# Routing of a mixture-of-experts layer: GpSimd's share moved to VectorE, the first tile's ranks moved behind the second tile's heads

## The chip, the cores and the metric

The kernel runs on one core of a Trainium2 chip. The metric is the device time of one execution, in microseconds (us); the median of several runs is compared. A core has five engines with instruction streams of their own: TensorE (PE in the profile; PEld is its weight load), VectorE (DVE), ScalarE (ACT), GpSimd (POOL) and SyncE (SP), whose queue issues most of the loads. Each takes its instructions in the order of the program; they wait for each other by semaphores.

## The reference

Two transformer blocks in a row, each of two layers, on 256 tokens of width 1024, in float32. The first (retention and stick-breaking attention, SwiGLU) is not touched. Of a layer of the second this matters:

```python
x = layer_norm(DEEPNORM_ALPHA * x + mix, ln1_g[l], ln1_b[l])     # mix: three attentions, then w_o
moe = hier_moe(x, router_group_w[l], ...)
x = layer_norm(DEEPNORM_ALPHA * x + moe, ln2_g[l], ln2_b[l])

def hier_moe(...):
    lg = einsum('td,dg->tg', t, rg_w) + rg_b                      # 4 groups
    g_hot = one_hot(argmax(lg)); p_top = sum(softmax(lg) * g_hot)
    le = einsum('td,gde->tge', t, re_w) + re_b                    # 8 experts in each group
    top_v, top_i = lax.top_k(le of the group, 2)
    gate = g_hot * (p_top * softmax(top_v) at top_i)
    for g in range(4):
        h = silu(t @ w_gate[g]) * (t @ w_up[g])
        y = y + (h * gate) @ w_down[g]
```

## The kernel before

The 256 tokens are two tiles of 128 (`t` = 0, 1; NT = 2). Matrix products with large weights are three matmuls each (`mm3`, lines 189 to 191: weights split in a high part `whi` and a low part `wlo`, tokens in `hi` and `lo`).

`mix2` computes the attentions of a layer. Its last part runs over the two tiles: the heads of the dilated attention in two pairs (`dil_pair`: products of queries and keys on line 897, a masked map with its row sum on VectorE on line 900, exponentials on ScalarE on line 905, the scaling of the shares on line 649, transposes on line 652, products with the values on line 917), then the out-projection into two accumulators `acc` of 512 columns, eight steps `k` of three matmuls each (and one matmul with `alpha` times the old `h`, line 947). The matmuls of an out-projection that have their inputs early are issued among the heads' steps, as fillers for TensorE's waits.

Then layer norm 1 and the routing of the tile. `nrm.stat` takes the statistics of each `acc` (line 675). `rt.logits` copies `acc` to `raw` on ScalarE (line 1016), transposes it (line 252) and multiplies with the router's weights (line 1031); the norm is applied to the 40 logits afterwards. `rt.route` works on VectorE (lines 1055 to 1077): maximum, group, top two experts, and `sg`, whose first half marks the two experts of each token. `rt.rank` counts the tokens of each expert with a matmul with a triangular matrix (`strict`, line 1123; for tile 1 also `ones`, line 1122, on the marks of tile 0), and `rt.places` (line 1114) turns the ranks into the 0/1 matrix `P` that gathers tokens into the slots of the experts, 32 for each.

The function `rest` of a tile does the remainder: `features` normalizes `acc` into `h` and, in the transposed order that the gather wants, into `hi` (ScalarE, lines 1039 and 1040), and takes `lo` = `h` - `hi` on GpSimd (line 1041); `nrm.affine` multiplies `h` by the gain and adds the bias (line 693, the first 512 columns on GpSimd, the others on VectorE), and `gates` computes the gate weights (lines 1087 to 1101). For tile 0 it runs inside the loop, for tile 1 after `mix2`.

`moe` then gathers the tokens of each group of experts (`group`, matmuls on line 1178, taken out of PSUM into `xe` on lines 1048 and 1050), counts the tokens of the fullest expert (`rt.count`, read into registers by the engines as `most_i`, line 1340), and runs through eight steps, each with four experts: gate and up products (line 1206), hidden values (line 1226), down products. The expert weights are 96 tiles of 1 MB a layer, loaded on SP's queue in order (line 1161) into every buffer that has come free, among them `rowb`, the 1 MB that holds gain and bias of layer norm 1, and `raw`, `whi`, `wlo`, `wx`, `more`.

Pools and a scheduler set the order of the instructions on each engine out of the order of the code; `keep_in_program_order` holds an instruction at its place in the code, and `issue_after` keeps instructions behind a given one.

Of the kernel before, what the change touches and what calls it, by code (L numbers as in the profile page):

```python
# [29 lines left out]
PIECES = 4  # L30

# [71 lines left out]
def tile_fn(ctx: ExitStack, tc: tile.TileContext, a: dict, out: bass.AP, stop=None, start=1):  # L103
# [560 lines left out]
    class LayerNorm:  # L664
# [19 lines left out]
        def shift(self, mv, y):  # L684
            nb = sm.tile([128, 1], F32, name="lnb")
            nc.vector.scalar_tensor_tensor(nb, mv[:, 0:1], -1.0, y, op0=OP.mult, op1=OP.mult)
            return nb
# [25 lines left out]
    def mix2(l, xp, wx, x, last, tabs, rt, ahead):  # L713
# [237 lines left out]
        for t in range(NT):  # L951
            pair = [dil_pair(t, n) for n in range(2)]
            for n in (0, 1, 0, 1) if t == 0 else (0, 0, 1, 1):
                next(pair[n])
            for k in (0, 2, 4):
                for c in range(2):
                    out_proj(t, c, range(k, k + 2))
            for c in range(2):
                out_proj(t, c, range(6, 8))
                nrm.stat(t, c, acc[t, c])  # L960
            rt.logits(t, [acc[t, c] for c in range(2)])
            mv, y = nrm.stats(t)
            rt.route(t, mv, y)
            rt.rank(t)
            rt.first.append(rt.places(rt.ranks(t, 0, 2)))
            after = (t, [acc[t, c] for c in range(2)], y, nrm.shift(mv, y))

            def rest(t=t, after=after):
                rt.features(*after)
                nrm.affine(t, 0, nc.gpsimd)  # L970
                nrm.affine(t, 1, nc.vector)
                rt.gates(t)
            if t == 0:
                rest()
        return rest
# [3 lines left out]
    class Route:  # L979
# [32 lines left out]
        def logits(self, t, src):  # L1012

            raw = [self.xp.tile([128, 512], F32, name="raw", tag="dt", bufs=2) for c in range(2)]
            for c in range(2):
                nc.scalar.copy(raw[c], src[c])
            for c in range(2):
                self.half(t, c, raw[c])

        def half(self, t, c, r):  # L1020
# [7 lines left out]
            if c:  # L1028
                self.acc = ps.tile([128, 512], F32, name="rt", tag="at", bufs=PB["at"])[:, :NR]
                for k in range(8):  # L1030
                    nc.tensor.matmul(self.acc, self.xT[2 * t + k // 4][:, k % 4], self.rw[:, k], start=k == 0, stop=k == 7)

        def features(self, t, src, y, nb):


            hi, lo = self.xt[t] = new_x(t)
            for c in range(2):
# [3 lines left out]
                nc.gpsimd.tensor_tensor(lo[:, :, sp], h[t][:, sl].rearrange("t (p k) -> t k p", k=8), hi[:, :, sp].bitcast(F32), op=OP.subtract)  # L1041
# [76 lines left out]
        def rank(self, t):  # L1118

            rk = ps.tile([128, 512], F32, name="rk", tag="at", bufs=PB["at"])[:, :NE]  # L1120
# [4 lines left out]
            nc.vector.scalar_tensor_tensor(self.rk[t], self.sel[t], -1024.0, rk, op0=OP.mult, op1=OP.add)  # L1125

# [10 lines left out]
    def moe(l, xp, wx, rt, then, ahead):  # L1137
# [31 lines left out]
        def gather(xe, P, n, tags, label=None):  # L1169

            nk, todo = 8 // len(tags), []
            for i, tag in enumerate(tags):
                todo.append((i * nk, ps.tile([128, nk, n], F32, name=tag, tag=tag, bufs=PB[tag])))
            for t in range(NT):
                for k0, pg in todo:
                    for k in range(nk):
# [157 lines left out]
        for i in range(NU):  # L1334
            q = i % 2
            if q == 0:
                xe, PT, gs, rest = group(i // 2)
                if i == 0:
                    rt.count()
            most = nc.values_load(rt.most[0:1, i:i + 1], min_val=0, max_val=T, skip_runtime_bounds_check_because="a count of tokens")  # L1340
            xq, gq = xe[:, :, q * 128:(q + 1) * 128], gs[:, q:q + 1]
            if i < NU - 1:
# [6 lines left out]
                hq = gate_up(i, xq, gq, others, None if i else rest)  # L1349
# [70 lines left out]
    for l in range(DEPTH):  # L1420
# [9 lines left out]
        rest()  # L1430
        if stop == f"at{l}":
            return store()
# [12 lines left out]
        with tc.tile_pool(name=f"moe{l}", bufs=1) as xp:  # L1445
            moe(l, xp, wx, rt, then, ahead)
# [32 lines left out]
```

## Time and profile before

| | us |
|---|---|
| median of 3 runs | 1728.81 (1728.62 to 1729.09) |
| the profiled execution | 1728.63 |
| its span (first to last instruction) | 1726.8 |
| outside the span | 1.83 |
| mean granted TensorE clock, share of full speed | 0.946 |
| TensorE busy | 1578.6 (91%) |
| VectorE busy | 906.1 (52%) |
| ScalarE busy | 680.9 (39%) |
| GpSimd busy | 80.3 (5%) |

The busy shares are means over 1727 us with very different stages: the first block and the projections keep TensorE busy throughout, the two MoE stages (about 1064 to 1260 and 1488 to 1680) move weights at some 418 GB/s. The change lies in two stretches of some 60 us, one ahead of each MoE stage, so they are read from a timeline and from windows. A row of a timeline begins with start and duration; a last part in brackets says how long the engine had stood idle, and what ended that.

### The profile page before, as it was taken

What the parts mean: (1) busy time and instruction counts of PE and PEld (TensorE: products, weight loads), DVE (VectorE), ACT (ScalarE), POOL (GpSimd) and SP (SyncE); (2) the same over time, 40 slices, a digit from 0 to 9 for tenths busy, and PEclk for the clock granted to TensorE, in tenths of its full rate; (3) what the DMA queues carried; (4) which work ended last, traced back from release to release, by engine and by line L of the source; (5) the groups of instructions that cost most, each with busy time, mean ns of one, the idle gap of its engine ahead of it and who ended that gap; (6) DMA issues with size and microseconds to landing.
All of it is one profiled execution on the core that took longest, in us unless ns stands there. A gap on an engine that the chain in (4) does not pass through costs nothing. (4 is left out here: it accounts for less than half of the span.)

```text
span 1726.8 us, 24247 instructions
## 1 busy us (share of the span) xinstructions
PE 1578.6 (91%) x9468; PEld 1190.1 (69%) x9468; DVE 906.1 (52%) x1966; ACT 680.9 (39%) x1126; POOL 80.3 (5%) x102
## 2 busy tenths in 40 slices
PE   9999999999999999999999998777779999786785
PEld 8788888888878888888787775443358777443442
DVE  5757675545575666445478544222167845432132
ACT  6543454343644445434376633111036754211010
POOL 0000000000000000000300111000030011100000
PEclk9999999999999999999999988988889998898798
DMA  9354546465635455546445628999972744899992
GB/s 321 123 193 149 193 163 204 154 213 181 207 122 194 154 185 174 187 143 223 139 124 190 225 102 341 418 418 419 413 256 87 255 160 168 357 417 419 419 372 71
DMA packets 133988, 399.54 MB, mean 231 GB/s; under 512 B 8133, under 2 KB 36805, under 8 KB 110278
## 3 DMA queue, kind: packets, MB, share of 16 engines
q1 hardware_dynamic: 130096, 390.62, 62.2%
q10 hardware_dynamic: 3734, 6.82, 1.1%
q8 instruction: 97, 1.59, 0.4%
q14 instruction: 61, 0.50, 0.1%
HBM read 396.37 MB, written 1.05 MB: 230 GB/s over the span
## 5 line engine op out<-in xcount | busy, mean ns | idle before, releaser
L165 DVE TENSOR_TENSOR wlo<-raw,whi 128x2048 fp32r<-128x2048 f32 (+6 forms) x314 | 405.8, 1310 | 306.7 <-ACT whi L164 305.8
L189 PE MATMUL acc<-whi,x 128*128 128x512 f32 (+3 forms) x1248 | 484.6, 389 | 0.2 <-ACT x L243 0.2
L164 ACT CAST whi<-raw 128x2048 fp32r<-128x2048 f32 (+7 forms) x346 | 355.1, 1063 | 325.2 <-PE acc L191 273.4
L191 PE MATMUL acc<-whi,x 128*128 128x512 f32 (+3 forms) x1248 | 478.6, 384 | 0.1
L190 PE MATMUL acc<-wlo,x 128*128 128x512 f32 (+3 forms) x1248 | 478.4, 384 | 0.0
L189 PEld LDWEIGHTS acc<-whi,x 128*128 128x128 f32 x1248 | 237.7, 190 | 45.1 <-issue 4.3
L190 PEld LDWEIGHTS acc<-wlo,x 128*128 128x128 f32 x1248 | 237.8, 191 | 44.3 <-issue 4.1
L191 PEld LDWEIGHTS acc<-whi,x 128*128 128x128 f32 x1248 | 237.3, 190 | 43.3 <-issue 2.3
L1206 PE MATMUL at<-whi,xe 128*32 128x256 f32 x448 | 105.4, 444 | 18.8 <-DMA whi<-in_expert_w_gate_dram 14.8
L1226 DVE SCALAR_TENSOR_TENSOR hq<-hh,gs,at 128x256 f32<-128x256 f32 x16 | 10.5, 656 | 167.5 <-PEq L1351 114.1
L1206 PE MATMUL at<-wlo,xe 128*32 128x256 f32 x416 | 84.4, 423 | 8.4 <-ACTq L1346 4.0
L165 POOL TENSOR_TENSOR wlo<-raw,whi 128x416 fp32r<-128x416 f32 (+1 forms) x32 | 32.8, 1059 | 1062.3 <-ACT whi L164 1062.2
L190 PE MATMUL acc<-wlo,fh 128*128 128x512 f32 x176 | 70.0, 398 | 0.0
L191 PE MATMUL acc<-whi,fl 128*128 128x512 f32 x176 | 70.0, 397 | 0.0
L189 PE MATMUL acc<-whi,fh 128*128 128x512 f32 x176 | 69.9, 397 | 0.0
L1206 PE MATMUL at<-wx,xe 128*32 128x256 f32 x416 | 51.3, 429 | 17.7 <-PEq L1317 6.7
L1206 PEld LDWEIGHTS at<-whi,xe 128*32 128x32 f32 x448 | 43.4, 126 | 34.0 <-issue 16.4
L1239 ACT COPY hT<-ph 128x256 f32<-128x256 f32 x17 | 6.3, 372 | 151.6 <-PE ph L1233 142.8
L244 DVE TENSOR_TENSOR yl<-acc,yh 128x512 fp32r<-128x512 f32 x30 | 20.6, 687 | 86.3 <-ACT yh L243 86.3
L1206 PE MATMUL at<-more,xe 128*32 128x256 f32 x352 | 55.0, 443 | 11.2 <-DMA more<-in_expert_w_up_dram 6.8
L1206 PE MATMUL at<-raw,xe 128*32 128x256 f32 x320 | 52.5, 474 | 12.8 <-issue 5.7
L1206 PEld LDWEIGHTS at<-wlo,xe 128*32 128x32 f32 x416 | 35.1, 120 | 24.8 <-issue 7.7
(378 smaller groups left out, 2192.0 us busy)
## 6 DMA issues: line engine op xcount, KB each, us to landing
raw<-in_w_in_dram SPq DMA_DIRECT2D x55, 1024.0 KB, 5.2
raw<-in_w_gate_up_dram SPq DMA_DIRECT2D x40, 1024.0 KB, 5.2
raw<-in_w_down_dram SPq DMA_DIRECT2D x22, 1024.0 KB, 4.9
whi<-in_expert_w_gate_dram SPq DMA_DIRECT2D x16, 1024.0 KB, 14.0
raw<-in_w_in_dram SPq DMA_DIRECT2D x28, 512.0 KB, 4.1
wx<-in_expert_w_up_dram SPq DMA_DIRECT2D x14, 1024.0 KB, 17.4
wx<-in_expert_w_down_dram SPq DMA_DIRECT2D x14, 1024.0 KB, 7.1
wlo<-in_expert_w_up_dram SPq DMA_DIRECT2D x14, 1024.0 KB, 17.4
```

The source lines that it names most:

```text
L164: nc.scalar.copy(hi[:, s], raw[:, s])
L165: eng.tensor_tensor(lo[:, s], raw[:, s], hi[:, s].bitcast(F32), op=OP.subtract)
L189: nc.tensor.matmul(acc, xhi[:, kt], whi[:, k, c0:c1], start=first, stop=False)
L190: nc.tensor.matmul(acc, xhi[:, kt], wlo[:, k, c0:c1], start=False, stop=False)
L191: nc.tensor.matmul(acc, xlo[:, kt], whi[:, k, c0:c1], start=False, stop=last)
L244: nc.vector.tensor_tensor(lo, p, hi.bitcast(F32), op=OP.subtract)
L1206: nc.tensor.matmul(pu[r], xe[:, k, r], W[i][4 * m + u][:, k], start=k == 0, stop=k == 7, skip_group_check=True)
L1226: nc.vector.scalar_tensor_tensor(hq.rearrange("s k p -> s p k"), hh.rearrange("s (p k) -> s p k", k=2), gs, pu.rearrange("s (p k) -> s p k ...
L1239: nc.scalar.copy(hT, ph)
```

## The change

In the loop of `mix2`: the last out-projection steps of both halves come first, then `logits`, and the statistics read the copy `raw` in SBUF in place of `acc` in PSUM. `route` may begin only after the last step of the norm's statistics (`shifted`). `rank` and `places` of tile 0 and its two subtractions (`low`) no longer follow its routing; they are issued in the loop for tile 1, behind its heads and the first six steps of its out-projection. The subtractions run on VectorE. `rank` of tile 1 is preceded by nine matmuls of the identity with itself into unused columns of its bank. Tile 0's gates stay in their place; tile 1's gates and all eight affine instructions, now all on VectorE, are issued in `moe` after `rt.count()`. The first gather issues tile 0's matmuls after the logits of tile 1, and runs through tile 1's with all `hi` first, then `lo`, with each bank taken out as soon as it is complete.

```diff
         def shift(self, mv, y):
...
-            nc.vector.scalar_tensor_tensor(nb, mv[:, 0:1], -1.0, y, op0=OP.mult, op1=OP.mult)
+            self.shifted = nc.vector.scalar_tensor_tensor(nb, mv[:, 0:1], -1.0, y, op0=OP.mult, op1=OP.mult)
...
                     out_proj(t, c, range(k, k + 2))
+            if t:
+
+                for low in lows:
+                    low()
+                rt.place(0)
             for c in range(2):
                 out_proj(t, c, range(6, 8))
-                nrm.stat(t, c, acc[t, c])
-            rt.logits(t, [acc[t, c] for c in range(2)])
+            raw = rt.logits(t, [acc[t, c] for c in range(2)])
+            for c in range(2):
+                nrm.stat(t, c, raw[c])
             mv, y = nrm.stats(t)
-            rt.route(t, mv, y)
-            rt.rank(t)
-            rt.first.append(rt.places(rt.ranks(t, 0, 2)))
-            after = (t, [acc[t, c] for c in range(2)], y, nrm.shift(mv, y))
-
-            def rest(t=t, after=after):
-                rt.features(*after)
-                nrm.affine(t, 0, nc.gpsimd)
-                nrm.affine(t, 1, nc.vector)
+            nb = nrm.shift(mv, y)
+            with tc.issue_after(nrm.shifted.ins):
+                rt.route(t, mv, y)
+
+            lows = rt.features(t, [acc[t, c] for c in range(2)], y, nb)
+            if t == 0:
                 rt.gates(t)
-            if t == 0:
-                rest()
-        return rest
+            else:
+                lows[0]()
+                rt.place(t)
+                lows[1]()
+
+        def affine():
+            for t in range(NT):
+                for c in range(2):
+                    nrm.affine(t, c, nc.vector)
+        return lambda: rt.gates(1), affine
...
+            def low(c):
+                sl, sp = slice(c * 512, (c + 1) * 512), slice(c * 64, (c + 1) * 64)
+                tc.keep_in_program_order(nc.vector.tensor_tensor(lo[:, :, sp], h[t][:, sl].rearrange("t (p k) -> t k p", k=8), hi[:, :, sp].bitcast(F32), op=OP.subtract))
...
-                nc.gpsimd.tensor_tensor(lo[:, :, sp], h[t][:, sl].rearrange("t (p k) -> t k p", k=8), hi[:, :, sp].bitcast(F32), op=OP.subtract)
+            return [lambda c=c: low(c) for c in range(2)]
...
         def rank(self, t):
...
+            rk = ps.tile([128, 512], F32, name="rk", tag="at", bufs=PB["at"])
+            if t:
+
+                for _ in range(SPIN):
+                    tc.keep_in_program_order(nc.tensor.matmul(rk[:, 128:256], ident, ident, start=True, stop=True, skip_group_check=True))
...
+        def place(self, t):
+            self.rank(t)
+            self.first.append(self.places(self.ranks(t, 0, 2)))
...
+            first = len(set(tags)) > 1
+            for t in range(NT):
+                if t and first:
+
+                    for u in range(2):
+                        for k0, pg in todo:
+                            for k in range(nk):
+                                nc.tensor.matmul(pg[:, k], xt[t][u][:, k0 + k], P[t], start=False, stop=u == 1, skip_group_check=True)
+                            if u:
+                                rt.evacuate(xe, pg, k0, nk)
+                    continue
                 for k0, pg in todo:
-                    for k in range(nk):
+                    with tc.issue_after(rt.logit.ins) if first and not t else nullcontext():
+                      for k in range(nk):
...
                 if i == 0:
                     rt.count()
+                    for f in rest:
+                        f()
```

How this moves instructions, at three places of the first layer. TensorE, between the out-projection of tile 0 and the heads of tile 1 (`x_7735` is tile 1's input to its out-projection, `dT` are queries and keys of the dilated heads, `sg_8000` the marks of tile 0), before:

```order
L191 MATMUL acc<-whi,x_7735 128x512
L947 MATMUL acc<-h_71,tabalpha 128x512
L189 MATMUL acc<-whi,x_7735 128x512
L190 MATMUL acc<-wlo,x_7735 128x512
L191 MATMUL acc<-whi,x_7735 128x512
L189 MATMUL acc<-whi,x_7735 128x512
L190 MATMUL acc<-wlo,x_7735 128x512
L1123 MATMUL rk<-sg_8000,tabstrict 128x32
L897 MATMUL at<-dT_7249,dT_7250 128x128
L897 MATMUL at<-dT_7251,dT_7252 128x128
L897 MATMUL at<-dT_7253,dT_7254 128x128
L897 MATMUL at<-dT_7250 128x128
```
The same place after the change (`x_7734` is tile 0's input, `tp` its transposes and `rt` its logits, lines 254 and 1044 of the new code):

```order
L193 MATMUL acc<-whi,x_7734 128x512
L254 MATMUL tp<-tabident,raw 128x128 x4
L949 MATMUL acc<-h_71,tabalpha 128x512
L254 MATMUL tp<-tabident,raw 128x128 x4
L1044 MATMUL rt<-rw,xT_7943 128x40 x4
L899 MATMUL at<-dT_7249,dT_7250 128x128
L899 MATMUL at<-dT_7251,dT_7252 128x128
L1044 MATMUL rt<-rw,xT_7943 128x40 x4
L899 MATMUL at<-dT_7253,dT_7254 128x128
L899 MATMUL at<-dT_7250 128x128
```
The rank matmul and the out-projection steps that stood ahead of the heads are gone from there; the heads begin among the logits.

TensorE, from the end of tile 1's out-projection on, before (line 1178 is the gather, 1131 the count):

```order
L190 MATMUL acc<-wlo,x_7735 128x512
L191 MATMUL acc<-whi,x_7735 128x512
L1178 MATMUL acc<-P,x_8013 128x256
L1475 BRANCH_PREFETCH_HINT
L252 MATMUL tp<-tabident,raw 128x128 x4
L1178 MATMUL acc<-P,x_8013 128x256 x7
L1178 MATMUL po<-P,x_8013 128x256
L252 MATMUL tp<-tabident,raw 128x128 x4
L1031 MATMUL rt<-rw,xT 128x40 x4
L1122 MATMUL rk<-sg_8000,tabstrict 128x32
L1178 MATMUL po<-P,x_8013 128x256 x3
L1031 MATMUL rt<-rw,xT 128x40 x4
```
After (`L1141` are the constant matmuls, 1144 and 1145 the rank, 1215 tile 0's gather, 1157 the count, 1207 tile 1's gather):

```order
L254 MATMUL tp<-tabident,raw 128x128 x8
L1044 MATMUL rt<-rw,xT 128x40 x8
L1141 MATMUL rk<-tabident 128x128 x9
L1144 MATMUL rk<-sg_8002,tabstrict 128x32
L1215 MATMUL acc<-P,x_8006 128x256
L1515 BRANCH_PREFETCH_HINT
L1215 MATMUL acc<-P,x_8006 128x256 x7
L1215 MATMUL at<-P,x_8006 128x256 x4
L1145 MATMUL rk<-sg_8316,tabstrict 128x32
L1215 MATMUL po<-P,x_8006 128x256 x4
L1157 MATMUL acc<-sg_8002,tabstrict 128x32
L1157 MATMUL acc<-sg_8316,tabstrict 128x32
```
The logits moved ahead of tile 0's gather, and constant matmuls and gather now stand between them and tile 1's rank.

VectorE, from the rank of tile 1 on, before (`h_71` is tile 1, `few` and `e` are the gates, `xe` the gathered tokens):

```order
L1076 TENSOR_TENSOR sg_8318<-es_8319,gh_8308 128x32
L1125 SCALAR_TENSOR_TENSOR rk_8325<-sg_8318,rk 128x32
L1134 TENSOR_REDUCE most<-acc 128x8
L1114 TENSOR_TENSOR P<-tabstrict,rk_8325 128x128 x2
L693 TENSOR_TENSOR h_71<-h_71,rowb 128x512
L1090 RECIPROCAL few_8344<-few_8344 128x1
L1096 TENSOR_SCALAR few_8344<-few_8344 128x1
L693 TENSOR_TENSOR h_71<-h_71,rowb 128x512
L1097 RECIPROCAL few_8344<-few_8344 128x1
L1135 CAST most_i<-most 128x8
```
After, up to the load of the count into registers:

```order
L1116 TENSOR_TENSOR few_8441<-few_8441 128x1
L1117 TENSOR_SCALAR e_8314<-e_8314,few_8441 128x8
L1065 TENSOR_SCALAR xe<-acc,rgx 128x256 x2
L1065 TENSOR_SCALAR xe<-at,rgx 128x256
L1065 TENSOR_SCALAR xe<-po,rgx 128x256
L1118 SCALAR_TENSOR_TENSOR es_8317<-e_8314,few_8441 128x8
L1093 TENSOR_TENSOR sg_8316<-es_8317,gh_8306 128x32
L695 TENSOR_TENSOR h_70<-h_70,rowb 128x512 x4
L695 TENSOR_TENSOR h_71<-h_71,rowb 128x512 x4
L1379 TENSOR_LOAD most_i
```
The affine instructions of both tiles (line 693, now 695) moved from between the gates, and from tile 0's part of the loop, to behind the last evacuation of the gather.

## Rows read from the trace of the kernel before

**Rows 1.** Windows: length; busy of PE, PEld, DVE, ACT, POOL; PEclk, DMA share, GB/s

```profile
1008.00:1012.00 4.00, 1.40 (x6) 0.75 (x4) 3.79 (x12) 0.49 (x3) 3.92 (x4) 0.94 0.35 104
1012.00:1025.20 13.20, 11.99 (x41) 9.71 (x42) 7.90 (x35) 2.81 (x9) 0.53 (x1) 0.50 0.36 128
1025.20:1049.00 23.80, 20.72 (x164) 17.04 (x162) 11.97 (x41) 11.91 (x28) 3.41 (x3) 1.00 0.72 270
1049.00:1059.30 10.30, 6.80 (x40) 5.41 (x44) 7.55 (x28) 3.94 (x7) 2.06 (x2) 0.50 0.99 402
1060.00:1063.00 3.00, 2.13 (x40) 0.99 (x36) 0.00 (x0) 0.38 (x1) 0.00 (x0) 1.00 0.02 5
1160.00:1170.00 10.00, 6.42 (x60) 2.81 (x52) 0.66 (x1) 0.37 (x1) 0.00 (x0) 0.67 1.02 419
...
1434.80:1448.40 13.60, 12.29 (x41) 9.93 (x42) 8.00 (x36) 2.82 (x9) 0.63 (x1) 0.50 0.34 131
```
**Rows 2.** Timeline of PE, layer 0: tile 0's routing to tile 1's out-projection

```profile
1009.00 0.40 PE L190 MATMUL acc<-wlo,x 128*128 128x512 f32 x1
...
1013.21 0.61 PE L1123 MATMUL rk<-sg,tabstrict 128*128 128x32 f32 x2 [3.81 <-DVE few L1090]
...
1025.43 0.82 PE L652 MATMUL tp<-tabident,smx 128*128 128x128 f32 x6
...
1034.03 0.85 PE L652 MATMUL tp<-tabident,smx 128*128 128x128 f32 x6
...
1038.05 0.50 PE L190 MATMUL acc<-wlo,x 128*128 128x512 f32 x1
...
1040.49 0.40 PE L191 MATMUL acc<-whi,x 128*128 128x512 f32 x1
```
**Rows 3.** Timeline of DVE and POOL in the same stretch, tile 0's routing

```profile
1006.64 0.26 DVE L1055 SCALAR_TENSOR_TENSOR r_lg<-rfix,lmv,rt 128x40 f32<-128x40 f32 x1 [1.42 <-PE rt L1031]
...
1006.84 3.14 POOL L1041 TENSOR_TENSOR x<-h,x 128x512 fp32r<-128x512 f32 x2 [31.07 <-ACT h L1040]
...
1006.93 1.54 DVE L1056 SCALAR_TENSOR_TENSOR r_lg<-r_lg,rs_y,rfix 128x40 f32<-128x40 f32 x1
...
1008.99 1.01 DVE L1062 TENSOR_TENSOR gh<-tabstrict,ig 128x4 f32<-128x4 f32 x1
...
1010.03 1.21 DVE L1064 TENSOR_TENSOR r_le<-r_lg,gh 128x32 f32<-128x32 f32 x1
...
1011.87 0.68 DVE L1091 TENSOR_TENSOR few<-te 128x1 f32<-128x1 f32 x1
...
1012.87 0.19 DVE L1076 TENSOR_TENSOR sg<-es,gh 128x32 f32<-128x32 f32 x1
```
**Rows 4.** Timeline of DVE, PE and SP: tile 1's routing and the loads behind

```profile
1045.38 0.26 DVE L1055 SCALAR_TENSOR_TENSOR r_lg<-rfix,lmv,rt 128x40 f32<-128x40 f32 x1 [1.41 <-PE rt L1031]
...
1051.48 0.19 DVE L1076 TENSOR_TENSOR sg<-es,gh 128x32 f32<-128x32 f32 x1
...
1051.72 0.64 PE L1123 MATMUL rk<-sg,tabstrict 128*128 128x32 f32 x2 [5.69 <-DVE sg L1076]
...
1053.56 0.77 PE L1178 MATMUL acc<-P,x 128*128 128x256 f32 x2 [0.77 <-DVE P L1114]
...
1054.81 0.33 SPq L1161 DMA_DIRECT2D rowb<-in_expert_w_up_dram  x1
...
1062.25 0.33 SPq L1161 DMA_DIRECT2D raw<-in_expert_w_up_dram  x1
```
**Rows 5.** Instructions by line: count, duration min/median/max in ns, first and last start

```profile
L900 DVE CUSTOM_DVE_ANT_1 smx<-at,tabalpha x24: 535/556/560, 983.6 to 1455.2; 128x384 f32<-128x384 f32 x24
...
L693 DVE TENSOR_TENSOR h<-h,rowb x8: 681/683/684, 1014.0 to 1477.1; 128x512 f32<-128x512 f32 x8
...
L1226 DVE SCALAR_TENSOR_TENSOR hq<-hh,gs,at x16: 654/655/666, 1068.2 to 1705.6; 128x256 f32<-128x256 f32 x16
...
L370 DVE SCALAR_TENSOR_TENSOR rp<-acc,rs_y,tabcos x16: 456/475/481, 71.1 to 511.7; 128x256 f32<-128x256 f32 x16
```

More of the change, by code (lines that the diff above doesn't have):

```diff
@@ L1018, in logits @@
                 self.half(t, c, raw[c])
+            return raw
         def half(self, t, c, r):
@@ L1030, in half @@
                 for k in range(8):
-                    nc.tensor.matmul(self.acc, self.xT[2 * t + k // 4][:, k % 4], self.rw[:, k], start=k == 0, stop=k == 7)
+                    self.logit = nc.tensor.matmul(self.acc, self.xT[2 * t + k // 4][:, k % 4], self.rw[:, k], start=k == 0, stop=k == 7)
         def features(self, t, src, y, nb):
             hi, lo = self.xt[t] = new_x(t)
+            def low(c):
+                sl, sp = slice(c * 512, (c + 1) * 512), slice(c * 64, (c + 1) * 64)
+                tc.keep_in_program_order(nc.vector.tensor_tensor(lo[:, :, sp], h[t][:, sl].rearrange("t (p k) -> t k p", k=8), hi[:, :, sp].bitcast(F32), op=OP.subtract))
             for c in range(2):
@@ L1118, in rank @@
         def rank(self, t):
[L1120 removed]
+            rk = ps.tile([128, 512], F32, name="rk", tag="at", bufs=PB["at"])
+            if t:
+                for _ in range(SPIN):
+                    tc.keep_in_program_order(nc.tensor.matmul(rk[:, 128:256], ident, ident, start=True, stop=True, skip_group_check=True))
+            rk = rk[:, :NE]
             if t:
@@ L1135, in count, with moe @@
             nc.vector.tensor_copy(self.most, m)
-    def moe(l, xp, wx, rt, then, ahead):
+    def moe(l, xp, wx, rt, then, ahead, rest):
         srcs = [a[n][l].rearrange("g e a b -> (g e) a b") for n in ("expert_w_gate_2", "expert_w_up_2", "expert_w_down_2")]
@@ L1336, in moe @@
             if q == 0:
-                xe, PT, gs, rest = group(i // 2)
+                xe, PT, gs, others_slots = group(i // 2)
                 if i == 0:
                     rt.count()
+                    for f in rest:
+                        f()
             most = nc.values_load(rt.most[0:1, i:i + 1], min_val=0, max_val=T, skip_runtime_bounds_check_because="a count of tokens")
@@ L1348, in others @@
                         second.extend(further(i, beyond(CAP)))
-                hq = gate_up(i, xq, gq, others, None if i else rest)
+                hq = gate_up(i, xq, gq, others, None if i else others_slots)
                 load(12 * i + 8 + NB)
@@ L1429, in tile_fn @@
             rest = mix2(l, xp, wx, x, last[-1], tabs, rt, ahead)
-        rest()
         if stop == f"at{l}":
+            for f in rest:
+                f()
             return store()
@@ L1445, in tile_fn @@
         with tc.tile_pool(name=f"moe{l}", bufs=1) as xp:
-            moe(l, xp, wx, rt, then, ahead)
+            moe(l, xp, wx, rt, then, ahead, rest)
         if stop == f"moe{l}":
```

1 line of the change is left out of this document (added).

## The prediction

> **What bounds the kernel now.** I looked first at the granted clock by stretches, because the change lies in one place of each layer: from the end of tile 0's out-projection to the first expert. [...] Next I read TensorE's timeline. It ends its filler matmuls at 1009.4 and then stands still for 3.81 us until the rank matmul of tile 0 (L1123) runs at 1013.21 [rows 2]. The heads of tile 1 stand behind that matmul in TensorE's order, so they wait too; they then run at half clock. What L1123 waits for is the routing on VectorE, which takes from 1006.64 to 1013.06, 6.4 us for some 14 small instructions [rows 3]. Four of them are long, 1.54, 1.01, 1.21 and 0.68 us, while their neighbours of the same size take 0.19 to 0.26. All four read two operands in SBUF, and they overlap GpSimd's subtractions and half of its affine work, which begin at 1006.84 [rows 3]. So the stall is GpSimd's presence, not VectorE's work.
>
> The second stall has the same shape: tile 1's routing from 1045.38 to 1051.67, TensorE idle 5.69 us before L1123, the gather at half clock behind it [rows 1, 4]. But that stage ends otherwise. The loads of expert weights go through one queue in order; `rowb` is issued at 1054.81, after the last affine, and `raw` at 1062.25, after the gate product of the first experts [rows 4]. From there the experts run at the pace of the loads: in 1160 to 1170 the DMA share is 1.02 and TensorE is busy 6.42 of 10 us [rows 1]. Between them, from 1060 to 1063, the queue is empty (share 0.02). What the second stage is worth is therefore when loading resumes, not when TensorE gets on.
>
> **Stage A, tile 0's routing to the end of tile 1's out-projection.** Call E the end of the last out-projection matmul, 1040.49 + 0.40 = 1040.9 [rows 2].
>
> The change takes GpSimd's subtractions and affine out, and puts the rank matmul twelve matmuls before E. The routing without contention: 6.42 us less the excess of the four, 4.44 - 4 x 0.2 = 3.6, gives 2.8 us. TensorE no longer waits for it: the heads of tile 1 stand directly behind the logits. What they wait for next is VectorE, which now does routing, gates and the four softmax sums of the first pair interleaved. Its logits come a little earlier (the copies no longer wait for the statistics): about 1006.2 for 1006.64. From there 2.8 for the routing, 1.4 for the eight gate instructions (0.18 each), 2.4 for four head maps (0.556 each and a short read [rows 5]) and 0.6 for sums, reciprocal and first scaling: 7.2 us if nothing overlaps, about 6.1 if half of the rows begin 0.08 before their predecessor ends (an estimate). I take 6.6: the transposes of the first pair (L652 of before) start at 1012.8, bounds 1012.3 and 1013.4. They stood at 1025.43 [rows 2]. The fillers that cover this wait end at about 1011.9, so an idle time of 0.8 us stays, 0.4 to 1.5.
>
> From there I take before's own steps at full clock [rows 1, 2]: first to second transposes 1034.03 - 1025.43 = 8.6; to the end of the second pair's value products 1038.05 - 1034.03 = 4.0; then the matmuls that are left. Before there were eleven, 0.244 apart from first to last [rows 2] and 0.234 without the pause behind the first; now fewer are used up as fillers, so 25 are left, 5.85 us, and the rank matmul 0.15. E' = 1012.8 + 8.6 + 4.0 + 6.0 = **1031.4**, 9.4 us earlier. A second account agrees: 3.0 of 3.8 us idle gone, and 13.2 us at half clock that cost 6.6.
>
> What moves into this stage: tile 0's two subtractions on VectorE. They write in the natural order and read `h` with a stride. The nearest rows are 0.683 for a contiguous operation of the same size on VectorE, and 0.655 against 0.475 for a scattered and a contiguous one of 256 elements [rows 5], so 0.68 to 0.94 each by that ratio, and not above the 1.57 that GpSimd took. They lie, with tile 0's places, beside the 25 matmuls, and cost nothing; were VectorE still busy when the copies of tile 1 arrive, up to 0.5.
>
> [...]
>
> **Stage B, from E' on.** Logits end at +3.4, so routing starts at +3.75 (before +4.48), takes 2.8 for 6.3, and is ready at +6.5 for +10.8 [rows 4]. The nine constant matmuls and tile 0's gather, which now follows the logits, fill TensorE until +7.15; then rank, places (1.3, for 1.84 from L1123 to the gather at half clock [rows 4]) and tile 1's gather from +8.45 (before +12.7), its evacuation to +12.7, the first gate product to +14. That is 7 us earlier than before, relative to E. But all eight affine instructions now stand on VectorE behind the evacuation: 8 x 0.64 (0.683 less the overlap) from +13.1 to +18.2. `rowb` waits for the last of them: +18.3 for +13.9, and `raw` behind it. Its 1 MB takes 2.5 us at 419 GB/s [rows 1], so the stream stands at `raw` at +20.8 for +21.35. Stage B is worth **0.6**, not 7; bounds -0.5 (subtractions at 1.57, one of which stands before the places) and 1.5.
>
> [...]
>
> **Sum.** 2 x (9.4 + 0.6) = 20.0 us, against the profiled 1728.63: 1708.6. The median of the runs is 1728.81, 0.18 above; I leave that. A run of this kernel tells 0.2% (3.5 us) from no change.
>
> **Rivals.**
> 1. The clock falls all the same behind the first pair. For it: before, TensorE had stood idle for some 2 us when it fell (a mean of 0.94 over 1008 to 1012 puts the fall 0.5 us before 1012), and 0.8 us idle between heads and transposes of 128 columns remain. Against it: the second pair's wait lies in 1025.2 to 1049, where the clock stays 1.00 [rows 1]. It costs up to 13.2 / 2 = 6.6 in that layer: 1715.2 for one, 1721.8 for both.
> 2. The loads don't hold the experts. Then stage B gives its 7 us, 1728.6 - 2 x 16.4 = 1695.8. Against it stands the share of 1.02.
> 3. Slower: the clock falls at the first pair and does not come back before routing ends, in both layers. E' is then 1031.4 + 6.6 + 25 x 0.234 = 1043.9, 3.0 late; the constant matmuls and both gathers at half clock add some 5 (an estimate, their doubled time), so the load stream resumes at +25.8, 4.4 late: 7.4 per layer, 1743. It decides once more than 20 us of TensorE-bound work in a layer stand at half clock, since half of that is the gain of 10. For it: 25 matmuls on the end of the stage are exposed. Against it: before, the clock came back among such matmuls at 1025.2 [rows 1].
> 4. The change doesn't remove the wait but moves it: if VectorE takes routing, gates and tile 0's rest ahead of the head maps, the transposes start at 1014.5 and all moves by 1.7 per layer: 1712.
>
> **How the numbers follow.** The forecast (with rival 4 as its upper part) 0.56: 1706 to 1713. Clock falls in one layer 0.22, in both 0.07 (still faster by 0.4%). Loads don't hold 0.05. Slower, rival 3, 0.06. The rest, 0.04, is a gain that another wait eats up: no change. Faster 0.90, same 0.04, slower 0.06. The forecast and a fall in one layer, 0.78 together, reach from 1706 to 1716. I go down to 1703 for the bounds of the transposes and of stage B (0.5 and 0.9 us per layer more), and up to 1721 to take in most of the falls in both layers.
>
> **What would show it.** In the profile after, L1056's successor takes about 0.2 us; TensorE's idle time ahead of the first pair's transposes is near 1 us; the clock stays at 1.00 between 1012 and 1040 and in the routing of tile 1; E' near 1031.4 and 10 + 423 earlier in layer 1; `rowb` issued at E' + 18.3, and the queue full from there. The prediction is wrong if the clock falls behind the first pair, if the subtractions on VectorE take well over 1 us, or if `raw` is issued more than 1 us off E' + 18.7.

## The result, and the profile after

The changed kernel takes 1709.25 us (median of 4 runs, 1706.14 to 1713.45) against 1728.74: a ratio of 0.9882, 95% interval 0.9871 to 0.9894, so 1.2% faster. The forecast was 1708.6. Its profiled execution took 1707.89, with a span of 1706.1, 20.7 us less than before.

The clock by stretches of the first layer (columns as in [rows 1]):

```profile
1008.00:1012.00 4.00, 4.00 (x19) 2.96 (x19) 3.86 (x31) 3.47 (x12) 0.00 (x0) 1.00 0.00 0
1012.00:1025.20 13.20, 12.92 (x111) 10.01 (x110) 6.68 (x27) 6.87 (x20) 0.00 (x0) 1.00 0.44 169
...
1031.00:1049.00 18.00, 13.91 (x148) 11.31 (x145) 16.04 (x56) 8.62 (x17) 0.00 (x0) 1.00 0.98 409
1049.00:1059.30 10.30, 8.21 (x92) 4.86 (x96) 2.99 (x14) 0.96 (x2) 0.00 (x0) 0.83 0.91 345
```

The 13.2 us that stood at 0.50 before now stand at 1.00, and TensorE does 111 instructions in them for 41. Here is the timeline of the same layer, VectorE, TensorE and SP in one, from tile 0's routing to the loads behind tile 1's:

```profile
1006.62 0.25 DVE L1072 SCALAR_TENSOR_TENSOR r_lg<-rfix,lmv,rt 128x40 f32<-128x40 f32 x1 [0.47 <-PE rt L1044]
...
1007.52 0.26 DVE L1073 SCALAR_TENSOR_TENSOR r_lg<-r_lg,rs_y,rfix 128x40 f32<-128x40 f32 x1
...
1009.00 0.16 DVE L1079 TENSOR_TENSOR gh<-tabstrict,ig 128x4 f32<-128x4 f32 x1
...
1012.67 0.85 PE L654 MATMUL tp<-tabident,smx 128*128 128x128 f32 x6 [0.18 <-DVE smx L651]
...
1020.99 0.85 PE L654 MATMUL tp<-tabident,smx 128*128 128x128 f32 x6
...
1025.63 2.23 DVE L1053 TENSOR_TENSOR x<-h,x 128x512 fp32r<-128x512 f32 x2
...
1030.84 0.39 PE L193 MATMUL acc<-whi,x 128*128 128x512 f32 x1
...
1034.85 0.25 DVE L1072 SCALAR_TENSOR_TENSOR r_lg<-rfix,lmv,rt 128x40 f32<-128x40 f32 x1
...
1037.46 0.19 DVE L1093 TENSOR_TENSOR sg<-es,gh 128x32 f32<-128x32 f32 x1
1037.57 1.17 DVE L1053 TENSOR_TENSOR x<-h,x 128x512 fp32r<-128x512 f32 x1
...
1039.51 0.71 PE L1207 MATMUL acc<-P,x 128*128 128x256 f32 x4 [0.33 <-DVE P L1131]
...
1043.85 5.39 DVE L695 TENSOR_TENSOR h<-h,rowb 128x512 f32<-128x512 f32 x8
...
1049.27 0.33 SPq L1187 DMA_DIRECT2D rowb<-in_expert_w_up_dram  x1
1050.45 0.37 SPq L1187 DMA_DIRECT2D raw<-in_expert_w_up_dram  x1
```

Against [rows 2, 3]: the instruction that took 1.54 us takes 0.26, the one with 1.01 takes 0.16. TensorE waits 0.18 us ahead of the first pair's transposes, which start at 1012.67 (forecast 1012.8) for 1025.43. The out-projection of tile 1 ends at 1030.84 + 0.39 = 1031.23 (forecast 1031.4) for 1040.89. Against [rows 4]: tile 1's routing takes 2.8 us for 6.3, and the gather starts 8.3 us behind the out-projection (forecast 8.45) for 12.7. The eight affine instructions end at 18.0, `rowb` goes out at 18.04 (forecast 18.3) and `raw` at 19.2 (forecast 18.7).

Two distances will compare all kernels, since they don't depend on when the stage begins: from the first routing instruction of tile 0 (`r_lg<-rfix`) to the end of tile 1's out-projection, called A, and from there to the issue of `rowb` and of `raw`. In the kernel before A is 34.25 us in the first layer and 34.42 in the second; in the changed kernel 24.61 and 24.61.

### The profile page after: what moved, and what is told of

It is laid out like the page before. It is cut to its first block, busy times and chain, and to the rows that moved or that the text cites. A ratio compares the mean times of both kernels' runs of the same rounds, so it can differ in the third digit from the quotient of the medians.

```text
span 1706.1 us, 24310 instructions
## 1 busy us (share of the span) xinstructions
PE 1563.5 (92%) x9504; PEld 1182.4 (69%) x9504; DVE 904.7 (53%) x1982; ACT 679.3 (40%) x1126; POOL 58.1 (3%) x86
## 3 DMA queue, kind: packets, MB, share of 16 engines
q8 instruction: 97, 1.59, 0.4%
## 5 line engine op out<-in xcount | busy, mean ns | idle before, releaser
L1243 PE MATMUL at<-whi,xe 128*32 128x256 f32 x448 | 99.4, 422 | 16.4 <-DMA whi<-in_expert_w_gate_dram 12.8
L1243 PE MATMUL at<-wlo,xe 128*32 128x256 f32 x416 | 82.1, 423 | 18.8 <-DVEq L1385 8.9
L1243 PE MATMUL at<-wx,xe 128*32 128x256 f32 x416 | 53.7, 436 | 19.9 <-issue 7.2
L1243 PE MATMUL at<-raw,xe 128*32 128x256 f32 x320 | 47.5, 438 | 10.9 <-PEq L1385 6.4
## 6 DMA issues: line engine op xcount, KB each, us to landing
wx<-in_expert_w_up_dram SPq DMA_DIRECT2D x14, 1024.0 KB, 19.7
wlo<-in_expert_w_up_dram SPq DMA_DIRECT2D x14, 1024.0 KB, 19.8
```

Of the source, the lines that this page charges most:

```text
L1243: nc.tensor.matmul(pu[r], xe[:, k, r], W[i][4 * m + u][:, k], start=k == 0, stop=k == 7, skip_group_check=True)
```

## Where the gain reached the end, and where it did not

Taken by layers the 20.7 us look different from the forecast's 10 + 10. From tile 0's routing in the first layer (1006.64 before, 1006.62 after) to the same place in the second the changed kernel is 6.2 us faster (1429.54 - 1006.64 = 422.9 for 1423.36 - 1006.62 = 416.7), from there to the end of the span 14.5 (1726.8 - 1429.54 = 297.3 for 1706.1 - 1423.36 = 282.7), although the stage gives 9.6 and 9.8 in them. What evens this out lies at the end of the expert stages. TensorE's queue comes three times in the program to the branch ahead of a further round (`rounds`); the first time closes the expert stage of the first layer, the last time that of the second (the second time lies within the second layer and took 6.0 us before, 7.5 after). Here are the branch and the event that follows it, before and after, by source line: count, duration min/median/max in ns, first and last start:

```profile
L1317 PEldq COMPARE_BRANCH  x3: 443/5955/6617, 1237.0 to 1682.9; - x3
L1317 PEldq EVENT_SEMAPHORE  x3: 51/51/51, 1237.5 to 1689.6; - x3
```

```profile
L1354 PEldq COMPARE_BRANCH  x3: 842/5935/7491, 1226.5 to 1669.6; - x3
L1354 PEldq EVENT_SEMAPHORE  x3: 51/51/51, 1232.5 to 1670.5; - x3
```

The branch of the first layer begins at 1237.0 before and is through at 1237.5, at 1226.5 after and through at 1232.5: 0.4 and 5.9 us. In the second layer it is the other way round: 6.6 before (1682.9 to 1689.6), 0.8 after. Nothing was changed there. So the first layer loses some 5.5 us of its gain and the second wins 5.8, and the edits of the change are not at these places; the two happen to cancel. The eleventh experiment is on this.

The branches are not all. From the end of the out-projection to the start of this last branch the first layer took 196.1 us before and 195.3 after, the second 219.0 and 221.6: there the second layer lost 2.7 us. Behind the branches the layers won another 1.2 and 1.6. So 6.2 is 9.6 + 0.8 - 5.5 + 1.2 but for rounding, and 14.5 is 9.8 - 2.7 + 5.8 + 1.6. The 2.7 belong to this one profile: in e1 and e10, which are the same kernel, the second layer takes 218.9 and 218.8 to its last branch. What lengthened it here was not traced.

## The experiments

All were compared with the kernel before on the same chip; the last column is the time over that of before with its interval. The branch column gives the first and the last branch of the two rows above.

| kernel | A, layers 1, 2 | to `rowb` | to `raw` | branch | median | ratio |
|---|---|---|---|---|---|---|
| before | 34.25, 34.42 | 13.9, 13.9 | 21.4, 21.3 | 0.4, 6.6 | 1728.74 | |
| changed | 24.61, 24.61 | 18.0, 18.0 | 19.2, 19.0 | 5.9, 0.8 | 1709.25 | 0.9882 (0.9871 to 0.9894) |
| e1, the same | 24.61, 24.63 | 18.0, 18.0 | 19.2, 19.0 | 6.1, 0.8 | 1710.04 | 0.9882 (0.9863 to 0.9901) |
| e2 rank early | 25.95, 25.93 | 18.0, 18.0 | 18.4, 18.5 | 6.2, 0.7 | 1706.19 | 0.9862 (0.9844 to 0.9881) |
| e3 subtractions on GpSimd | 25.82, 25.81 | 19.8, 20.7 | 21.0, 21.7 | 6.1, 1.1 | 1715.80 | 0.9916 (0.9898 to 0.9934) |
| e4 engine alone | 27.39, 27.38 | 12.1, 12.1 | 19.9, 20.7 | 0.4, 6.6 | 1710.30 | 0.9885 (0.9867 to 0.9903) |
| e5 no constant matmuls | 24.62, 24.64 | 18.6, 19.2 | 19.7, 20.2 | 0.4, 5.1 | 1712.49 | 0.9908 (0.9892 to 0.9925) |
| e6 affine split | 24.63, 24.63 | 15.4, 15.4 | 17.6, 16.3 | 0.4, 0.5 | 1704.57 | 0.9863 (0.9847 to 0.9880) |
| e7 four | 24.63, 24.62 | 18.5, 18.8 | 19.7, 19.8 | 5.9, 0.6 | 1704.46 | 0.9863 (0.9846 to 0.9879) |
| e8 eighteen | 24.63, 24.65 | 17.7, 17.7 | 18.9, 18.7 | 6.0, 6.2 | 1709.27 | 0.9884 (0.9866 to 0.9902) |
| e9 = e6 | 24.62, 24.63 | 15.4, 15.4 | 17.1, 16.4 | 0.4, 1.1 | 1703.84 | 0.9854 (0.9830 to 0.9878) |
| e10 = changed | 24.64, 24.63 | 18.0, 18.0 | 19.2, 19.0 | 6.0, 0.7 | 1707.61 | 0.9864 (0.9839 to 0.9889) |
| e11 before, shifted | 34.27, 34.46 | 13.9, 13.9 | 21.2, 21.3 | 6.0, 0.6 | 1725.54 | 0.9969 (0.9952 to 0.9986) |
| e12 early and split | 25.98, 26.02 | 15.4, 15.4 | 17.5, 16.4 | 5.9, 1.3 | 1702.84 | 0.9835 (0.9809 to 0.9861) |

**e1: the same kernel again.** No edit.

> The changed kernel once more, for its spread. The four runs so far lie from 1706.1 to 1713.5 us, those of before within 0.5. If the spread comes from the granted clock in the expert stages (theory), both stages ahead of them end where they did, the out-projection of tile 1 at 1031.2 and 1447.8 relative to the start within 0.3 in the first layer, while the end of the expert stage of the first layer moves by up to 4 us. If it comes from the routing (rival), the first out-projection itself ends more than 1 us away from 1031.2.

The stage has the same length to 0.02 us, but it began at 1010.74 for 1006.62, so the out-projection ended at 1035.35. That is the sign which the rival had named, but not its cause: the routing is as long as before, and both spoke of absolute times. By the start times of ScalarE's instructions, 2.6 us of the difference are there within the first 20 us of the program, and the rest arises between 867 us and 911 us, ahead of tile 0's routing. Nor does it all last: the second layer is 2.8 us shorter than in the first profile of the same kernel, and the span is only 2.2 longer. So executions of one kernel differ by some microseconds ahead of the change's place and behind it; the kernel before shows such a spread as well in the runs beside the experiments (1723 to 1734 beside e9 to e12). This is why the stage is judged by distances below, and times only by ratio.

**e2: rank, places and subtractions of tile 0 back behind its routing.**

```diff
-            if t:
-
-                for low in lows:
-                    low()
-                rt.place(0)
             for c in range(2):
                 out_proj(t, c, range(6, 8))
...
             if t == 0:
+                rt.place(0)
+                for low in lows:
+                    low()
                 rt.gates(t)
```

> The changed kernel with the rank, places and subtractions of tile 0 back directly behind its routing; VectorE still does all of it. Theory A (the gain comes from GpSimd's absence: uncontended routing takes 2.8 us and is done when the fillers end): the rank matmul waits less than 0.7 us, the clock stays at 1.00, out-projection of tile 1 ends at 1031 to 1032, time 1706 to 1714. Theory B (the order is what counts, heads must not stand behind the rank): TensorE idles over 2 us again, the clock falls, the out-projection ends at 1036 or later, time 1719 or more.

Theory A. The rank matmul stands in the old place, but it waits for next to nothing:

```profile
1009.98 0.40 PE L192 MATMUL acc<-wlo,x 128*128 128x512 f32 x1
1010.34 0.38 PE L1143 MATMUL rk<-sg,tabstrict 128*128 128x32 f32 x2
```

The filler ends at 1010.38, and the matmul starts at 1010.34; the clock is 1.00 throughout. A is 25.9 us, so the out-projection would end at 1032.6 if tile 0's routing had begun at 1006.6 (1031 to 1032 was expected). With VectorE doing the work, the rank's new place is worth 1.3 us a layer of the 9.7, and none in the measured time.

**e3: subtractions on GpSimd again.**

```diff
-                tc.keep_in_program_order(nc.vector.tensor_tensor(lo[:, :, sp], ...
+                nc.gpsimd.tensor_tensor(lo[:, :, sp], ...
```

> The changed kernel with the four subtractions of a layer back on GpSimd, directly behind the norm; affine stays on VectorE, order as changed. Theory A: VectorE's routing takes 3 us longer again, now in front of the shares of the first pair, so the transposes start at about 1015.7 for 1012.7 and TensorE idles some 3 us: out-projection ends at 1034.3 if the clock holds, up to 1040 if it falls; tile 1's routing takes 5.5 to 6 us. Time 1715 to 1726. Theory B: the order alone carries the gain, time 1706 to 1714.

Between the two. Contention is back:

```profile
1011.63 3.13 POOL L1057 TENSOR_TENSOR x<-h,x 128x512 fp32r<-128x512 f32 x2 [31.75 <-DVE r_lg L1073]
...
1012.80 0.41 DVE L905 TENSOR_TENSOR dnm<-dnm 128x1 f32<-128x1 f32 x1
...
1013.21 0.54 DVE L902 CUSTOM_DVE_ANT_1 smx<-at,tabalpha 128x384 f32<-128x384 f32 x1
...
1013.69 1.12 DVE L1081 TENSOR_TENSOR r_le<-r_lg,gh 128x32 f32<-128x32 f32 x1
...
1017.73 0.52 PE L654 MATMUL tp<-tabident,smx 128*128 128x128 f32 x3 [1.38 <-DVE smx L651]
...
1045.03 0.41 PE L1145 MATMUL rk<-sg,tabstrict 128*128 128x32 f32 x2 [1.84 <-DVE sg L1093]
```

In the first stage it costs 1.2 us and not 3: the head maps, which read PSUM, run through beside GpSimd, and only two instructions are held up, the 0.41 and the 1.12, which take 0.15 and 0.18 in the changed kernel. TensorE waits 1.38 us ahead of the transposes for 0.18, and the clock holds. In the second stage tile 1's rank waits 1.84 us and `raw` is issued 1.7 and 2.7 us later. The time, 1715.8, lies in the range of theory A (1715 to 1726); the share of each stage was not expected.

**e4: the engine alone.** The kernel before, with `nc.vector` for `nc.gpsimd` in its two lines (1041 and the call of `affine`).

> The kernel before with its GpSimd work of this place (subtractions and half of affine) on VectorE, and nothing else changed; the scheduler puts subtractions and affine among the routing. Theory A: no instruction of the routing takes over 0.3 us, but 2.2 us of subtractions and 0.6 of affine stand in front of the marks, so the rank matmul waits 1 to 2 us instead of 3.8 (six more fillers stand ahead of it); if the clock holds, most of the first stage's gain is there, out-projection end at 1032 to 1034, and the time is 1708 to 1717. Theory B: out-projection end at 1038 or later, time 1722 or more.

Theory A. TensorE waits 1.15 us where it waited 3.81:

```profile
1013.69 0.38 PE L1123 MATMUL rk<-sg,tabstrict 128*128 128x32 f32 x2 [1.15 <-DVE few L1090]
```

The clock stays at 1.00 from 1009 to 1036, and A is 27.4, and the out-projection ended at 1035.8, which is 1034.0 if tile 0's routing had begun at 1006.6 as before. Two words in the code give 6.9 of the 9.6 us of the first stage. The ratio, 0.9885, is that of the whole change, which the stages don't explain: they give 6.9 and 7.0 us, in place of 9.6 and 9.8, with the last branches as in the kernel before. The profiled execution was the slowest of the four (1714.45 for a median of 1710.30), so where the others won the rest is not shown.

**e5, e7, e8: none, four and eighteen constant matmuls** (`SPIN = 0`, `4`, `18`).

> The changed kernel without its nine constant matmuls (18 instructions of TensorE per layer, since each counts twice). In the stage itself: tile 1's places wait for VectorE, which has a subtraction of 1.17 us ahead of them, so TensorE idles some 1.5 us but the gather starts where it did, 8.3 us behind the out-projection, rowb is issued 18.0 behind it, and the clock stays at 1.00 (theory); rival: the clock falls ahead of the gather, and rowb comes 1.5 us or more later. Behind it, theory C: which of TensorE's branches take 4 to 7 us and which 0.4 depends on where they stand in its instruction stream; with the 18 and 36 instructions gone, the last branch of the first expert stage takes 0.4 and that of the second 6 to 7 us, as in the kernel before, in place of 6 and 0.8. Rival to C: it depends on how long the loads keep the DMA queues busy, and the pattern stays that of the changed kernel. Time 1704 to 1712 either way, since the two last branches trade places.

> The changed kernel with four constant matmuls in place of nine (8 instructions per layer in place of 18). The stage: as with nine, rowb 18.0 us behind the out-projection. Theory C (position in the instruction stream): the long branches fall on other places than with nine or with none for at least one of the two last branches, and the time moves by up to 6 us with no difference in the stage. Rival: same pattern as with nine.

> The changed kernel with 18 constant matmuls in place of nine. They take 4.4 us in place of 2.2 and end behind tile 1's marks, so tile 1's rank waits about 1 us and tile 0's gather (1.9 us) stands behind it: places and gather 2 us later, affine behind them too, rowb 19 to 20 us behind the out-projection. Theory (the load stream has a gap of some 2 us there and decides): 1 to 2 us a layer lost, 2 to 4 in all, beside what the branches do. Rival: the stage is hidden behind the loads and nothing but the branches changes.

Without them TensorE idles 0.78 us ahead of the rank and 1.07 behind it (1.60 of 3.3 us busy), and the clock falls at the gather:

```profile
1037.20:1040.50 3.30, 1.60 (x12) 1.52 (x13) 3.23 (x12) 2.58 (x7) 0.00 (x0) 1.00 1.00 415
1040.60:1043.90 3.30, 3.30 (x26) 2.39 (x28) 2.29 (x9) 1.93 (x4) 0.00 (x0) 0.50 1.00 417
```

So the rival of e5 was right on the clock, and about half as dear as it said: `rowb` 0.5 and 1.2 us later. Four give 0.5 and 0.8. Eighteen cost nothing and win 0.3, where 1 to 2 us of loss were expected: the rank that waits for them does wait (tile 0's gather stands behind it), but part of the affine work then runs ahead of the evacuations, and what `rowb` waits for is the end of VectorE's work (1049.15, `rowb` at 1049.18), not of TensorE's. On theory C: with none, the last branches are 0.4 and 5.1 as in the kernel before (6 to 7 was expected for the second). With four they are as with nine, so the rival of e7 held for these two, though another branch at 1145 took 0.34 us for 4.6; with eighteen both are long. The times (0.9908, 0.9863, 0.9884) do not follow the stage: with four it is worse than with nine, and the time is no longer. (The profile without constant matmuls is of its fastest execution, 1706.85 for a median of 1712.49; the branches of the slower ones are not seen.)

**e6, e9: tile 0's subtractions and affine in VectorE's idle stretches.**

```diff
             PT = [[shares(x, ...
+            if t and n == 0:
+                for low in lows:
+                    low()
+            if t and n == 1:
+                for c in range(2):
+                    nrm.affine(0, c, nc.vector)
...
         def affine():
-            for t in range(NT):
-                for c in range(2):
-                    nrm.affine(t, c, nc.vector)
+            for c in range(2):
+                nrm.affine(1, c, nc.vector)
```

> The changed kernel with tile 0's two subtractions between the two head pairs of tile 1, and tile 0's four affine instructions behind the second pair's shares, where VectorE stood idle for about 3 us each. Theory: the first stage stays at 24.6 us from tile 0's logits to the end of tile 1's out-projection; four affine instructions fewer stand behind the gather, rowb is issued 15.3 us behind the out-projection for 18.0, and the gap of about 2 us in the load stream closes: 2 us a layer, time 3 to 4 us below that of the changed kernel on the same chip. Rival: the branch of TensorE behind the first gate product (3.7 to 4.6 us by itself) holds all engines as long as the affine instructions did, so less than 1 us is gained per layer.

> The variant with subtractions and affine of tile 0 in VectorE's idle stretches once more, on the same chip as the changed kernel itself (next run). Theory: 15.3 us again from the out-projection to rowb (18.0 in the changed kernel), time 3 to 5 us below that of the changed kernel on this chip. Its last branch of the first expert stage took 0.44 us in the first look, where the changed kernel with the same count of instructions took 6: if that is a property of the program, it is 0.4 again; if chance, it may be 6, with about 4 us more time.

```profile
1014.38 2.09 DVE L1055 TENSOR_TENSOR x<-h,x 128x512 fp32r<-128x512 f32 x2
...
1022.87 2.74 DVE L695 TENSOR_TENSOR h<-h,rowb 128x512 f32<-128x512 f32 x4
...
1044.40 2.74 DVE L695 TENSOR_TENSOR h<-h,rowb 128x512 f32<-128x512 f32 x4
...
1047.17 0.33 SPq L1189 DMA_DIRECT2D rowb<-in_expert_w_up_dram  x1
1049.40 0.33 SPq L1189 DMA_DIRECT2D raw<-in_expert_w_up_dram  x1
```

The stage did what was expected to 0.1 us: A unchanged, `rowb` at 15.4 for 18.0; `raw`, which SP issues behind the branch that follows the first gate product (TensorE is through it at 1049.26), gains 1.6 and 2.7. The medians are 1704.6 and 1703.8, 3.8 us below the changed kernel's 1707.6 on the same chip, though the intervals of the ratios overlap. Not all of it is the stage: in both profiles of this program the first layer's branch is short (0.4 us for 6.0).

**e10: the changed kernel beside it.**

> The changed kernel beside it. Stage: 24.6 us from tile 0's logits to the out-projection's end, rowb 18.0 behind it; last branches of the two expert stages about 6 and 0.8 us, as in its two looks so far. Time 1706 to 1712, ratio to before 0.988.

As expected: 24.64, 18.0, 6.0 and 0.7, and a ratio of 0.9864 (0.9839 to 0.9889).

**e11: the kernel before, shifted by nine constant matmuls at its very start.**

```diff
-            spin(10)
+            spin(19)
```

> The kernel before with nine more constant matmuls at the very start of the program (19 in place of 10), so that all of TensorE's later instructions stand 18 places further on; the stages of the change are untouched, and the time of both (34.3 us from logits to out-projection end) stays. Theory C (a branch's time depends on its place in TensorE's stream): the last branch of the first expert stage goes from 0.44 to about 6 us, that of the second from 6.6 to under 1.1; which ones are long changes although nothing near them did, and the time by up to 5 us either way. Rival: the branches follow the stage's timing, and stay at 0.44 and 6.6.

```profile
L1317 PEldq COMPARE_BRANCH  x3: 632/5999/6057, 1239.2 to 1686.8; - x3
L1317 PEldq EVENT_SEMAPHORE  x3: 51/51/51, 1245.3 to 1687.5; - x3
```

Theory C. The two branches change places, 6.0 and 0.6 for 0.4 and 6.6, a thousand microseconds behind the edit, with both stages of the change as they were (34.27, 13.9, 21.2). The kernel even becomes 0.3% faster (0.9952 to 0.9986). The two branches are not all that moved: the second layer's experts reach the last branch 214.5 us behind the out-projection, for 219.0 before, and what shortened that was not traced.

**e12: early rank and split affine together.**

> The rank of tile 0 in its old place (directly behind the routing, as in the second experiment), all on VectorE, and tile 0's affine instructions behind the second pair's shares. Theory: 25.9 us for the first stage, rowb 15.3 us behind it, so 1.3 us a layer behind the variant with the late rank and 1.4 ahead of the changed kernel; time 1700 to 1708 by its branches. Rival (the order of the rank matters after all): over 1709.

The theory, in each number (25.98 and 26.02, 15.4). At 1702.84 and 0.9835 it is the fastest by its median; from e9 on the same chip (0.9854, 0.9830 to 0.9878) it is not told apart.

## Why the prediction was right

**The wait was GpSimd's, and it cost the clock.** The forecast took 3.0 us of idle time and 6.6 us of half clock off the first stage; A shrank by 9.6 and 9.8. What it did not see is that its two causes do not add. By A: the kernel before 34.3; the engine alone changed 27.4 (e4); the whole change with the rank in its old place 25.9 (e2); the whole change with the subtractions on GpSimd 25.8 (e3); the whole change 24.6. The rank's place is worth 1.3 once VectorE does the work, and the engine of the subtractions 1.2 once the rank stands late, while the whole is worth 9.6. Most of the price is the clock: it stood at 0.50 for 13.2 us before, which is 6.6 us, and is 1.00 throughout A in e2, e3, e4 and the changed kernel. So the forecast's "takes GpSimd's subtractions and affine out, and puts the rank matmul twelve matmuls before E" names two edits, of which the first alone gives 6.9 us. That the second alone would do as much is not shown: in e3 affine stays off GpSimd, and no run has the new order with all of GpSimd's work. Nor were the change's other edits, which lie between e4 and e2 (1.4 us), taken apart.

The 1.54 us of [rows 3] against the 0.26 of the instruction before it, which has an operand in PSUM, don't bear the contention alone, because the 0.26 began at 1006.64 and GpSimd only at 1006.84. What bears it are the 0.26 of the same instruction without GpSimd (1007.52 above), and e3, where head maps with an operand in PSUM keep their 0.54 us beside GpSimd.

**The working of stage A.** Routing was to start 0.44 us earlier; it did not (1006.62 for 1006.64). The copies do begin 0.49 earlier (1001.13 for 1001.62), but the matmuls with `alpha` and four of the heads now stand on TensorE among the transposes and logits, so the last logits end at 1006.59 as before (1006.61), and it is for them that VectorE waits (`[0.47 <-PE rt L1044]`). VectorE's chain took 6.05 us to the transposes, below the 6.1 to 7.2 given. The two errors cancel, and the idle time left was 0.18 for 0.8. The steps behind were read off before's rows and came out as read: 8.32 for 8.6, then 4.0, then 6.2 for 6.0.

**The subtraction.** 0.68 to 0.94 us were given; 1.12 to 1.18 were measured in all eight:

```profile
L1053 DVE TENSOR_TENSOR x<-h,x x8: 1117/1144/1178, 1025.6 to 1456.0; 128x512 fp32r<-128x512 f32 x8
```

```profile
L165 DVE TENSOR_TENSOR wlo<-raw,whi 128x512 fp32r<-128x512 f32 x112 | 75.1, 700 | 28.6 <-ACT whi L164 27.9
```

That is 1.7 times the contiguous 0.683, where the scattered and the contiguous row of 256 elements gave a ratio of 1.4 [rows 5]; the scattered one writes with a stride, while this one reads with one. The output type is not the reason: a contiguous subtraction into the same type takes 0.70 on average in the kernel before (the second row). That the subtractions take "well over 1 us" was one of the forecast's signs of being wrong; 1.12 to 1.18 comes near it. That the stride is what the 0.46 us more (1.144 for 0.683) come from is not shown, since no run varies it. They cost next to nothing: tile 0's pair lies beside the out-projection, and tile 1's first holds up the places by at most the 0.33 us that TensorE waits ahead of the gather.

**Stage B** was to give 0.6, and the affine instructions to hold `rowb`: 18.04 for 18.3. `raw` came 0.5 us later than forecast: it stands behind a branch which TensorE took 3.7 us for and VectorE reached only after the affine instructions. By the forecast's own count (`rowb` and 2.5 us for its megabyte) the stream stands at 20.5 for 21.4, 0.8 us, and in the first layer 0.8 us is what the last branch comes earlier (196.1 for 195.3 behind the out-projection). In the second hardly any of it arrives: the last branch comes 2.7 us later in this profile, 0.1 and 0.2 earlier in e1 and e10. e6 shows that `rowb` could have gone out 2.7 us sooner, which the change spent on tile 0's four affine instructions.

**Rival 1** (the clock falls behind the first pair) never came, in any kernel without both GpSimd and the old order. Rival 2 (loads do not hold the experts) is refuted as stated: the gate product ended 14 us behind the out-projection for 21, and of these 7 us 0.8 were left at the last branch of the first layer and nothing at that of the second. But the premise it attacked is only nearly true: a branch of 6 us at the end of the expert stage does reach the end, as e11 shows. Rival 3 needed the fall of rival 1, and rival 4 put the transposes at 1014.5, where they came at 1012.67.

**Sum.** 20.0 forecast, 20.7 by the spans, 19.5 by the medians. The mechanism of stage A is shown, and 19.4 of the 20.7 are A's. That the sum is this close owes something to chance all the same: the branches took 5.5 us in one layer and gave 5.8 in the other, and the 2.7 us that the second layer's experts lost are made up for by the 2.8 won behind the branches, which nobody forecast.

## What to carry to other kernels

When short instructions of an engine are long only while another engine works, move the other's work before reordering anything: two words gave here 6.9 of the stage's 9.6 us. Ask of each microsecond of a TensorE wait whether it also costs the clock: here 13.2 us at 0.50 were 6.6 of the 9.6, and the two remedies for that one wait did not add, each worth 1.2 to 1.3 us where the other stood. And compare variants of a program with branches by the stage that was edited: here nine matmuls at the very start changed which of the later branches are long (6.0 and 0.6 us for 0.4 and 6.6), and that edit alone was worth 0.3% (e11).

## What the runs showed of the hardware

The last branch of TensorE in an expert stage takes 0.4 to 1.3 us in some programs and 5.1 to 6.6 us in others, much the same at each of the two places in each profile of one program (changed kernel, e1, e10; e6 and e9), and which places are long changes with instructions added or left out far ahead (e11, e5). In the traces of the kernel before and of the changed one, the long ones go with packets of one DMA queue. The DMA view of a window counts packets by queue (packets, MB, share of 16 engines), and gives one, q8, the kind `instruction`, with packets of 16 KB (97 packets and 1.59 MB in the whole program, in both). In the changed kernel, ahead of the first layer's last branch (1216 to 1226.5) and during it (1226.6 to 1232.4):

```profile
q1 hardware_dynamic: 608, 4.42, 101.1%
...
q1 hardware_dynamic: 324, 2.36, 99.2%
q8 instruction: 1, 0.02, 1.1%
```

In the kernel before, ahead of the same branch (1232.5 to 1237.0) and during it (1237.0 to 1237.4):

```profile
q1 hardware_dynamic: 261, 1.88, 101.1%
q8 instruction: 1, 0.02, 1.4%
...
q1 hardware_dynamic: 20, 0.16, 98.1%
```

By the start times of the packets, the one in the kernel before starts 4.1 us ahead of this branch and takes 1.0, and the branch takes 0.44 us; the one in the changed kernel starts 3.4 us after the branch has begun and takes 1.0, and the branch takes 5.9. All 21 branches of TensorE of 1.4 us or more in these two profiles (6 before, 15 after) end 1.3 to 1.7 us behind the end of such a packet; of the 41 below 0.5 us, 4 end 1.4 to 1.8 us behind one. That a long branch waits for such a packet is the author's reading of these times; no run moves a packet by itself. The place in the stream is not all that decides: the edit of e6 and e9 moves instructions of VectorE alone, and yet their first branch takes 0.4 us for 5.9 in the changed kernel. Why stays open.

During the branch of 6 us TensorE does next to nothing (0.26 us busy from 1226.6 to 1232.4), and the clock stood at 0.50 for the last products of the first layer's experts:

```profile
1230.50:1240.70 10.20, 5.44 (x52) 2.40 (x56) 0.00 (x0) 0.00 (x0) 0.00 (x0) 0.50 1.01 404
```

Also unexpected: while GpSimd's subtractions run, VectorE's head maps, with one operand in PSUM, take their usual 0.54 to 0.56 us, and of the others in the first stage of e3 only two, both with all operands in SBUF, take longer (0.41 for 0.15 and 1.12 for 0.18), so that an interleaved order left 1.2 us of contention there, for 3.6 in the kernel before.
